# Last 256 output columns of a decoder layer: another order of token blocks, the residual added in PSUM, and the first norm's root one step earlier

## The chip, the cores and the metric

The kernel runs on one core of a Trainium2 chip. The metric is the device time of one execution in microseconds (us); the verdict compares the medians of several runs. One further execution is recorded by the profiler, and all durations of single instructions come from it. Engines are written as in the profile: PE (matrix multiply), PEld (its weight loads), DVE (vector), ACT (scalar and activation), POOL, and SP, which here only issues DMAs. ACT and POOL issue DMAs too.

## What is computed

One decoder layer over 320 tokens of width 2048: 256 of a prompt and 64 of a sample (8 sequences of 8). In the reference, cut to what matters here:

```
xn = rms_norm(x, g_mix);  z = xn @ w_in        # B, C, h, q, k, v and two gates
h  = x + merged(conv branch, window attention) @ w_o
hn = rms_norm(h, g_ffn)
h  = h + (silu(hn @ w_gate) * (hn @ w_up)) @ w_down      # inner width 5632
y  = rms_norm(h, g_final)                                # y_prompt, y_sample
```

Caches of keys, values and convolution state are returned as well. All is float32 in and out.

## The kernel before, in words

**Layout.** Activations are held transposed: 128 of the 2048 features on the partitions, 320 tokens along the free axis, 16 blocks of features. `hT` is the residual in that form. Tokens come in three blocks, `TOK`: 0-127 and 128-255 of the prompt and the 64 of the sample.

**Products.** A weight tile of 512 rows by 256 columns is loaded by SP into `wraw` (L98), copied by ACT into a rounded half `whi` (L93) and subtracted by DVE into the rest `wlo` (L94). `product` (L116) runs three matmuls for each 128x128 piece (whi with the rounded activations, whi with their rest, wlo with the rounded ones) into two PSUM buffers of 128 features by 320 tokens. The group that PE's time is made of is L134.

**Order.** Every engine has a queue that it works through in order. The framework fixes these queues at build time, from what is ready, and among the ready by the order of the program. `after(...)` (L71) ties an instruction behind marked ones of the same engine. Small work beside a product is written as a generator; `tick` advances it by one `yield` for each weight tile, with all that it issues tied behind the last matmul, the last whi and the last wlo traced so far.

**Start.** `x_load(i)` (L223) loads a group of feature blocks of x in three pieces, one for each block of tokens: all on SP but the first group's second piece, which is on ACT, followed there by g_mix (`vrow`, L231). Nine matmuls on ones warm PE up (L235). `kv_product` (L268) is the first real product: keys and values, 512 columns, nine tiles of 1, 1 and seven times 2 feature blocks. `x_prep` transposes a block of x on PE (L246), scales it on ACT into `xh_t` (L247) and on DVE into `xl_t` (L248), and copies it to `hT` (L253). `start_rest` (L327) is the side work: small loads, sums of squares, and at its end the root of the first norm (`rstd_of`, L178, with `inv_root`, L185 to L190), three diagonal matrices `dg` (L367) and three matmuls `prb` (L368) that spread the root over all partitions. The last six k/v matmuls are tied behind `prb`. Then `rb` is copied out of PSUM (L376), and kT and vT are scaled by it (L378, L380). The q product follows; behind its fourth tile SP issues two large copies of the caches from DRAM to DRAM (L427).

**End.** The inner width is worked in halves of 24 and 20 blocks. In the second half the first seven column pairs of w_down are products as above; then `to_rows` transposes each finished block back to token rows (L935), ACT sums squares (L929), and DVE multiplies by g_final into the row buffers `y_sb` (L965). At the first of these pairs `rows_so_far` also transposes blocks 14 and 15, to which this half has not been added yet, and copies them to `y_sb` (L946). The last 256 columns are computed the other way round, tokens on the partitions: `row_product(t)` (L992) gives 128 tokens by 256 columns in PSUM, 60 matmuls for a prompt block, 40 for the sample (its rounded half and its rest lie side by side as 128 rows). `finish_row` (L1010) adds the residual from `y_sb` on DVE (L1013, for the sample a second time, L1015), sums the squares, and computes the root of the final norm. The loop at L1023 takes the blocks in the order prompt 0, prompt 1, sample, scales the rows and sends them: two sends for a prompt block (512 KB each), three for the sample.

Where `inv_root` is called with one column per row it is five short steps with a change of engine on both sides of the root:

```
last["root"] = nc.scalar.activation(s, v, AF.Sqrt)
nc.vector.reciprocal(r, s)
nc.vector.scalar_tensor_tensor(s, r, -0.5, r, op0=ALU.mult, op1=ALU.mult)
nc.vector.tensor_mul(s, s, v)
```

The functions that the change touches, with the line numbers of the profile:

Of the kernel before, what the change touches and what calls it, by code (L numbers as in the profile page):

```python
# [40 lines left out]
def hybrid_layer(ctx: ExitStack, tc: tile.TileContext, a: dict, o: list):  # L41
# [133 lines left out]
    def rstd_of(ss, shape, name, pool, out=None):  # L175

        v = pool.tile(shape, F32, tag=f"rs_v{shape[1]}", name=u(name))
        nc.vector.tensor_scalar(v, ss, 1.0 / D, EPS, op0=ALU.mult, op1=ALU.add)  # L178
        return inv_root(v, shape, name, pool, out)
# [43 lines left out]
    def x_load(i):  # L223
        cs = slice(sum(XB[:i]) * P, sum(XB[:i + 1]) * P)
        for t, (t0, tn) in enumerate(TOK):
            src = a["x_prompt"][0, t0:t0 + tn, :] if t < 2 else a["x_sample"].flatten_outer_dims()
            eng = nc.scalar if i == 0 and t == 1 else nc.sync
            eng.dma_start(xs[t][:tn, cs], src[:, cs])

    x_load(0)  # L230
    nc.scalar.dma_start(vrow[0:16, :], a["g_mix"][0].rearrange("(k p) -> k p", p=P))  # L231

    wm = ps_aux("wm")
    for _ in range(9):
# [92 lines left out]
    def start_rest():  # L327
        yield
        small_loads()
        yield  # L330
        squares(0)
        yield
        yield
        squares(1)
        pw = ps_aux("pw")
        nc.tensor.transpose(pw[:, 0:56], vrow, ident[:56, :56])
        nc.vector.tensor_copy(vecs[:, 16:56], pw[:, 16:56])
        yield
        squares(2)
        nc.vector.tensor_scalar(nsink, sink_bc, -1.0, None, op0=ALU.mult)  # L340
        pe_ = ps_aux("pe_")
        nc.tensor.matmul(pe_[:NH, :WIN], rel, oh, start=True, stop=True)
        e_sb = st.tile([NH, EL], F32, name="e_sb")
        nc.vector.memset(e_sb, NEG)
        nc.vector.tensor_copy(e_sb[:, WIN - 1:2 * WIN - 1], pe_[:NH, :WIN])
        nc.gpsimd.dma_start(e_scr, e_sb)
        yield
        squares(3)
        s3 = st.tile([P, 3], F32, name="s3")
        nc.vector.tensor_reduce(s3, ss, axis=AX.X, op=ALU.add)  # L350
        pst = ps_aux("pst")
        for c in range(8):
            nc.tensor.transpose(
                pst[:, c * 16:(c + 1) * 16], srow[:, c * P:(c + 1) * P], ident[:16, :16]
            )
        nc.vector.tensor_copy(st_sb.rearrange("p c s -> p (c s)"), pst[:, 0:128])
        nc.gpsimd.dma_start(
            bias_s, bass.AP(e_scr.tensor, e_scr.offset + WIN - TS, [[EL, NH], [1, TS], [1, WIN + TS]])
        )
        yield  # L360
        yield
        r3 = rstd_of(s3, [P, 3], "r3", st)
        prb = ps_aux("prb")
        mark["rb"] = prb
        for t, (t0, tn) in enumerate(TOK):
            dg = st.tile([P, P], F32, name=f"dg{t}")
            nc.vector.tensor_scalar(dg[:tn, :tn], ident[:tn, :tn], r3[:tn, t:t + 1], None, op0=ALU.mult)  # L367
            mark["prb"] = nc.tensor.matmul(  # L368
                prb[:, t0:t0 + tn], ones[:tn, :], dg[:tn, :tn], start=True, stop=True
            )  # L370
# [507 lines left out]
    for half in range(2):  # L878
# [34 lines left out]
                    )  # L913
        if half == 1:
            ya = xp.tile([P, 2, D], F32, tag="xh", name="ya")
            yb = xp.tile([P, 2 * D + DC], F32, tag="xl", name="yb")
            y_sb = [ya[:, 0, :], ya[:, 1, :], yb[:, 0:D]]
            gfb = yb[:, D:2 * D]

            yo = yb[64:P, 2 * D:]  # L920
            nc.gpsimd.dma_start(gfb, a["g_final"].partition_broadcast(P))
            NSQ = KC - 1
            ssf = op.tile([P, 3, NSQ], F32, name="ssf")
            nc.vector.memset(ssf, 1.0)

            def row_squares(t, i, src):
                tn, n = TOK[t][1], src.shape[-1]
                jk = tmp("td", "jk")
                nc.scalar.activation(jk[:tn, :n], src, AF.Square, accum_out=ssf[:tn, t, i:i + 1])  # L929

            def to_rows(k):
                pt = ps_aux(u("fa"))
                dst = [pt[:tn, t * P:(t + 1) * P] for t, (t0, tn) in enumerate(TOK)]
                for t, (t0, tn) in enumerate(TOK):
                    nc.tensor.transpose(dst[t], hT[:, k, t0:t0 + tn], ident)  # L935
                return dst

            warm = op.tile([P, 1], F32, name="warm")
            with after(last["sig"]):
                nc.scalar.activation(warm, ones[:, 0:1], AF.Sqrt)  # L940

            def rows_so_far():

                for k in (KC - 2, KC - 1):
                    for t, src in enumerate(to_rows(k)):
                        nc.vector.tensor_copy(y_sb[t][:TOK[t][1], k * P:(k + 1) * P], src)  # L946

        for mp in range(8 if half == 0 else 7):
            c0 = mp * CW
            ps = product(  # L950
                lambda k0, n: load_cols(w_d, f0 + k0, n, c0), nf,
                lambda k: a_h[:, k, :], lambda k: a_l[:, k, :], "dn",
            )
            for c in range(2):
                k = mp * 2 + c
                nc.vector.tensor_add(hT[:, k, :], hT[:, k, :], ps[c][:, :T])
            if half == 1:
                pc = [to_rows(mp * 2 + c) for c in range(2)]
                for c in range(2):
                    k = mp * 2 + c  # L960
                    ks = slice(k * P, (k + 1) * P)
                    for t in range(3):
                        row_squares(t, k, pc[c][t])
                    for t, (t0, tn) in enumerate(TOK):
                        nc.vector.tensor_mul(y_sb[t][:tn, ks], pc[c][t], gfb[:tn, ks])  # L965
                if mp == 0:
                    rows_so_far()


    nf = FH[1]  # L970
# [21 lines left out]
    def row_product(t):  # L992

        ps = ps_acc(u("dr"))
        t0, tn = TOK[t]
        for k in range(nf):
            wh, wl = (w[:, k % KT, :] for w in held[k // KT])
            if t < 2:
                xhk, xlk = a_h[:, k, t0:t0 + tn], a_l[:, k, t0:t0 + tn]
                ms = ((xhk, wh), (xlk, wh), (xhk, wl))  # L1000
            else:
                both = a_t[:, k, t0:t0 + 2 * tn]
                ms = ((both, wh), (both, wl))
            for m, (x, w) in enumerate(ms):
                nc.tensor.matmul(  # L1005
                    ps[:, :CW], x, w, start=(k == 0 and m == 0), stop=(k == nf - 1 and m == len(ms) - 1)
                )
        return ps

    def finish_row(t, ps):  # L1010
        tn = TOK[t][1]
        y = y_sb[t][:tn, es]
        nc.vector.tensor_add(y, ps[:tn, :CW], y)  # L1013
        if t == 2:
            nc.vector.tensor_add(y, ps[tn:2 * tn, :CW], y)  # L1015
        row_squares(t, NSQ - 1, y)
        v = op.tile([P, 1], F32, name=u("vf"))
        nc.vector.scalar_tensor_tensor(
            v, ssf[:, t, NSQ - 1:NSQ], 1.0 / D, s14[:, t:t + 1], op0=ALU.mult, op1=ALU.add
        )  # L1020
        return inv_root(v, [P, 1], "rf", op)

    for t in range(3):  # L1023
        tn = TOK[t][1]
        y = y_sb[t]
        r = finish_row(t, row_product(t))[:tn]
        gl = gfb[:tn, es]
        if t < 2:
            out = y_p[0, t * P:(t + 1) * P, :]
            nc.scalar.activation(y[:, 0:DC], y[:, 0:DC], AF.Copy, scale=r)  # L1030
            nc.vector.tensor_scalar(y[:, DC:e0], y[:, DC:e0], r, None, op0=ALU.mult)
            nc.vector.scalar_tensor_tensor(y[:, es], y[:, es], r, gl, op0=ALU.mult, op1=ALU.mult)
            nc.sync.dma_start(out[:, 0:DC], y[:, 0:DC])
            nc.sync.dma_start(out[:, DC:D], y[:, DC:D])
        else:
            out = y_s.flatten_outer_dims()
            nc.scalar.activation(yo[:, 0:e0 - DC], y[:tn, DC:e0], AF.Copy, scale=r)
            h = DC // 2
            nc.vector.tensor_scalar(y[:tn, 0:h], y[:tn, 0:h], r, None, op0=ALU.mult)
            nc.sync.dma_start(out[:, 0:h], y[:tn, 0:h])  # L1040
            nc.vector.scalar_tensor_tensor(yo[:, e0 - DC:], y[:tn, es], r, gl, op0=ALU.mult, op1=ALU.mult)
            nc.scalar.dma_start(out[:, DC:D], yo)
            nc.vector.tensor_scalar(y[:tn, h:DC], y[:tn, h:DC], r, None, op0=ALU.mult)
            nc.sync.dma_start(out[:, h:DC], y[:tn, h:DC])


_INS = ['x_prompt', 'x_sample', 'cache_k', 'cache_v', 'state_conv', 'rel_bias', 'w_in', 'w_conv',
# [38 lines left out]
```

## Time and profile before

| | |
|---|---|
| median of 3 runs | 1701.68 us (1701.42 to 1701.92) |
| profiled execution, its own time | 1700.47 us |
| span in its profile, first to last instruction | 1698.7 us |
| granted TensorE clock, mean | 0.998 |
| PE busy | 1686.0 us, 11640 matmuls |
| DVE, ACT, POOL busy | 868.8, 644.6, 81.3 us |
| HBM read and written | 253.29 MB, 5.08 MB |

The profile's rows read: start (us from the span's start), duration (us), engine, line, operation, tiles written and read, shape, count, and in brackets the idle time of that engine just before, with what ended it. "q" behind an engine's name means that its queue issued a DMA. The waits list who waited for whom, and the chain is the sequence of work and waits that ended last.

### The profile page before, as it was taken

Reading aid. Unit: us, or ns where it says so; the run is one execution under the profiler, and the core shown is the slowest. Engines: PE = TensorE matmul, PEld = TensorE weight load, DVE = VectorE, ACT = ScalarE, POOL = GpSimd, SP = SyncE. Lnnn points to the kernel's source line nnn. Section 1 sums busy time; section 2 is a strip of 40 time slices with the busy share of each in tenths; the row PEclk is TensorE's granted clock in tenths of the full one; section 3 lists DMA queues with packets and bytes.
Section 4 is the critical chain, followed back from the end, with each engine's and each line's share of the span. In section 5 each row is a group of like instructions: output and inputs, shape, how many; then the busy total and the mean of one; then the engine's idle time right before and its main releaser. Section 6 shows DMA issues by size and latency. Waiting matters only on the chain.

```text
span 1698.7 us, 27819 instructions
## 1 busy us (share of the span) xinstructions
PE 1686.0 (99%) x11640; PEld 1673.2 (98%) x11640; DVE 868.8 (51%) x1259; ACT 644.6 (38%) x940; POOL 81.3 (5%) x127
## 2 busy tenths in 40 slices
PE   9999999999999999999999999999999999999997
PEld 8999999999999999999999999999999999999997
DVE  6667654444444445555454545433335555554444
ACT  6445443333333333334333333322233333333343
POOL 1001221000000001220000000000000000000000
PEclk9999999999999999999999999999999999999999
DMA  7654544554454444444444544444444444445443
GB/s 219 208 154 138 160 151 137 151 149 149 149 149 149 149 150 150 150 150 148 151 150 151 151 152 151 149 149 149 149 150 149 149 150 150 151 152 168 150 143 106
DMA packets 256654, 258.22 MB, mean 152 GB/s; under 512 B 9090, under 2 KB 251486, under 8 KB 256368
## 3 DMA queue, kind: packets, MB, share of 16 engines
q1 hardware_dynamic: 254144, 250.12, 47.6%
q0 software_dynamic: 2128, 5.92, 1.1%
q8 instruction: 91, 1.49, 0.4%
q10 hardware_dynamic: 256, 0.40, 0.1%
q14 instruction: 35, 0.29, 0.0%
HBM read 253.29 MB, written 5.08 MB: 152 GB/s over the span
## 4 chain that ended last, share of the span: by engine, by line
PE 97%; DVE 0%; issue 0%; ACT 0%; DVEq 0%; ACTq 0%
PE fu L134 18%; PE fg L134 18%; PE dn L134 17%; PE wo L134 7%; PE gc L134 7%; PE ga L134 7%; PE C L134 3%; PE B L134 3%; PE H L134 3%; PE ya L134 3%; PE yc L134 3%; PE q L134 3%; PE dr L1005 1%; PE fa L935 0%; PE po L518 0%; PE pp L505 0%
## 5 line engine op out<-in xcount | busy, mean ns | idle before, releaser
L94 DVE TENSOR_TENSOR wlo<-wraw,whi 128x1024 fp32r<-128x1024 f32 (+1 forms) x479 | 571.5, 1196 | 692.6 <-ACT whi L93 690.0
L93 ACT ACTIVATE whi<-wraw 128x1024 fp32r<-128x1024 f32 (+1 forms) x479 | 491.2, 1030 | 841.9 <-PE dn L134 192.1
L134 PE MATMUL dn<-a_t,whi 128*128 128x320 f32 x1328 | 293.4, 309 | 0.0
L134 PEld LDWEIGHTS dn<-a_t,whi 128*128 128x128 f32 x1328 | 221.5, 188 | 0.0
L134 PE MATMUL fu<-hh_t,whi 128*128 128x320 f32 x704 | 217.2, 309 | 0.0
L134 PE MATMUL fg<-hh_t,wlo 128*128 128x320 f32 x704 | 217.1, 308 | 0.0
L134 PE MATMUL fg<-hh_t,whi 128*128 128x320 f32 x704 | 217.1, 308 | 0.0
L134 PE MATMUL fg<-hl_t,whi 128*128 128x320 f32 x704 | 217.1, 308 | 0.0
L134 PE MATMUL fu<-hl_t,whi 128*128 128x320 f32 x704 | 217.0, 308 | 0.0
L134 PE MATMUL fu<-hh_t,wlo 128*128 128x320 f32 x704 | 217.0, 308 | 0.0
L134 PE MATMUL dn<-a_t,wlo 128*128 128x320 f32 x664 | 204.8, 308 | 0.0
L134 PEld LDWEIGHTS fu<-hl_t,whi 128*128 128x128 f32 x704 | 132.1, 188 | 0.1
L134 PEld LDWEIGHTS fu<-hh_t,whi 128*128 128x128 f32 x704 | 132.1, 188 | 0.1
L134 PEld LDWEIGHTS fg<-hl_t,whi 128*128 128x128 f32 x704 | 132.1, 188 | 0.0
L134 PEld LDWEIGHTS fg<-hh_t,wlo 128*128 128x128 f32 x704 | 132.1, 188 | 0.0
L134 PEld LDWEIGHTS fg<-hh_t,whi 128*128 128x128 f32 x704 | 132.1, 188 | 0.0
L134 PEld LDWEIGHTS fu<-hh_t,wlo 128*128 128x128 f32 x704 | 132.1, 188 | 0.0
L134 PEld LDWEIGHTS dn<-a_t,wlo 128*128 128x128 f32 x664 | 124.6, 188 | 0.0
L134 PE MATMUL gc<-xh_t,whi 128*128 128x320 f32 x256 | 79.5, 311 | 0.0
L134 PE MATMUL ga<-xh_t,whi 128*128 128x320 f32 x256 | 79.4, 310 | 0.0
L134 PE MATMUL ga<-xl_t,whi 128*128 128x320 f32 x256 | 79.4, 310 | 0.0
L134 PE MATMUL ga<-xh_t,wlo 128*128 128x320 f32 x256 | 79.4, 310 | 0.0
(298 smaller groups left out, 2851.3 us busy)
## 6 DMA issues: line engine op xcount, KB each, us to landing
wraw<-in_w_in_dram SPq DMA_DIRECT2D x119, 512.0 KB, 3.7
wraw<-in_w_gate_dram SPq DMA_DIRECT2D x88, 512.0 KB, 3.6
wraw<-in_w_up_dram SPq DMA_DIRECT2D x88, 512.0 KB, 3.6
wraw<-in_w_down_dram SPq DMA_DIRECT2D x88, 512.0 KB, 3.5
wraw<-in_w_o_dram SPq DMA_DIRECT2D x32, 512.0 KB, 3.5
wraw<-in_w_in_dram SPq DMA_DIRECT2D x34, 256.0 KB, 4.3
wraw<-in_w_conv_out_dram SPq DMA_DIRECT2D x16, 512.0 KB, 3.5
wraw<-in_w_attn_out_dram SPq DMA_DIRECT2D x32, 256.0 KB, 3.9
```

The lines of the kernel that those rows point to most:

```text
L93: last["hi"] = nc.scalar.activation(hi, src, AF.Copy)
L94: last["lo"] = nc.vector.tensor_sub(lo, src, hi.bitcast(F32))
L134: last["mm"] = nc.tensor.matmul(ps[c][:, :T], w[:, k, c * P:(c + 1) * P], x(kc), start=(kc == 0 and i == 0), stop=(kc == nk - 1 and i == 2),)
L1005: nc.tensor.matmul(ps[:, :CW], x, w, start=(k == 0 and m == 0), stop=(k == nf - 1 and m == len(ms) - 1))
```

## The change

Three parts.

- **The end.** The blocks go in the order prompt 0, sample, prompt 1. `rows_so_far` is gone. Instead `row_product` begins, for a prompt block, by transposing the residual of blocks 14 and 15 straight into the PSUM buffer, and the product accumulates on it; for the sample the two transposes go through another PSUM buffer and DVE copies them to `y_sb`. `finish_row` sums squares from PSUM for the prompt blocks, without adds. The first two blocks are sent in two pieces each; the last one, now a prompt block, in four, all on SP. The sample no longer has a second row buffer.
- **The root.** `rstd_of` for the first norm stands one `yield` earlier; `dg` and `prb` stay where they were.
- **The loads.** The sample's pieces of the first two groups of x are issued by ACT instead of SP, and g_mix is issued ahead of the first pieces of x.

```diff
-            eng = nc.scalar if i == 0 and t == 1 else nc.sync
+            eng = nc.scalar if (i, t) in ((0, 1), (0, 2), (1, 2)) else nc.sync
...
+    nc.scalar.dma_start(vrow[0:16, :], a["g_mix"][0].rearrange("(k p) -> k p", p=P))
     x_load(0)
-    nc.scalar.dma_start(vrow[0:16, :], a["g_mix"][0].rearrange("(k p) -> k p", p=P))
...
         yield
-        yield
         r3 = rstd_of(s3, [P, 3], "r3", st)
+        yield
         prb = ps_aux("prb")
...
-                if mp == 0:
-                    rows_so_far()
...
         ps = ps_acc(u("dr"))
         t0, tn = TOK[t]
+        for c in range(2):
+            res = hT[:, KC - 2 + c, t0:t0 + tn]
+            if t < 2:
+                nc.tensor.matmul(
+                    ps[:, c * P:(c + 1) * P], res, ident, start=c == 0, stop=False, is_transpose=True
+                )
+            else:
+                pt = ps_aux(u("fa"))
+                nc.tensor.transpose(pt[:tn, 0:P], res, ident)
+                nc.vector.tensor_copy(y_sb[t][:tn, e0 + c * P:e0 + (c + 1) * P], pt[:tn, 0:P])
...
-                    ps[:, :CW], x, w, start=(k == 0 and m == 0), stop=(k == nf - 1 and m == len(ms) - 1)
+                    ps[:, :CW], x, w, start=(t == 2 and k == 0 and m == 0),
+                    stop=(k == nf - 1 and m == len(ms) - 1),
...
-        y = y_sb[t][:tn, es]
-        nc.vector.tensor_add(y, ps[:tn, :CW], y)
+        y = ps[:tn, :CW]
         if t == 2:
+            y = y_sb[t][:tn, es]
+            nc.vector.tensor_add(y, ps[:tn, :CW], y)
             nc.vector.tensor_add(y, ps[tn:2 * tn, :CW], y)
...
+    for t in (0, 2, 1):
...
+        mul = lambda a0, a1: nc.vector.tensor_scalar(y[:, a0:a1], y[:, a0:a1], r, None, op0=ALU.mult)
+        act = lambda a0, a1: nc.scalar.activation(y[:, a0:a1], y[:, a0:a1], AF.Copy, scale=r)
+        send = lambda a0, a1: nc.sync.dma_start(out[:, a0:a1], y[:, a0:a1])
+        if t == 1:
+            mul(0, 256)
+            act(1024, 1408)
+            send(0, 256)
+            send(1024, 1408)
+            mul(256, 1024)
+            act(1408, e0)
+            send(256, 1024)
         else:
...
+            mul(0, 1024)
+            act(1024, e0)
+            send(0, 1024)
+        nc.vector.scalar_tensor_tensor(y[:, es], yl, r, gl[:tn], op0=ALU.mult, op1=ALU.mult)
+        send(1408 if t == 1 else 1024, D)
```

More of the change, by code (lines that the diff above doesn't have):

```diff
@@ L360, in start_rest @@
         yield
+        r3 = rstd_of(s3, [P, 3], "r3", st)
         yield
-        r3 = rstd_of(s3, [P, 3], "r3", st)
         prb = ps_aux("prb")
@@ L915, in hybrid_layer @@
             ya = xp.tile([P, 2, D], F32, tag="xh", name="ya")
[L916 to L920, printed above, removed]
+            yb = xp.tile([P, 2, D], F32, tag="xl", name="yb")
+            y_sb = [ya[:, 0, :], ya[:, 1, :], yb[:, 0, :]]
+            gfb = yb[:, 1, :]
             nc.gpsimd.dma_start(gfb, a["g_final"].partition_broadcast(P))
@@ L940, in hybrid_layer @@
                 nc.scalar.activation(warm, ones[:, 0:1], AF.Sqrt)
[L942 to L946, printed above, removed]
         for mp in range(8 if half == 0 else 7):
@@ L1020, in finish_row @@
         )
-        return inv_root(v, [P, 1], "rf", op)
-    for t in range(3):
+        return y, inv_root(v, [P, 1], "rf", op)
+    gl = gfb[:, es]
+    for t in (0, 2, 1):
         tn = TOK[t][1]
[L1025 to L1034, printed above, removed]
-        else:
[L1036 to L1044, printed above, removed]
+        y = y_sb[t][:tn]
+        yl, r = finish_row(t, row_product(t))
+        r = r[:tn]
+        out = y_p[0, t * P:(t + 1) * P, :] if t < 2 else y_s.flatten_outer_dims()
+        mul = lambda a0, a1: nc.vector.tensor_scalar(y[:, a0:a1], y[:, a0:a1], r, None, op0=ALU.mult)
[9 more added lines that the diff above has]
+            send(256, 1024)
+        else:
+            mul(0, 1024)
[3 more added lines that the diff above has]
+        send(1408 if t == 1 else 1024, D)
 _INS = ['x_prompt', 'x_sample', 'cache_k', 'cache_v', 'state_conv', 'rel_bias', 'w_in', 'w_conv',
```

## The prediction

> **What bounds the kernel now.** I read the page first, for what is busy; then the rows of PE in order of time, for where it isn't; then the chain at each such place.
>
> ```profile
> PE 1686.0 (99%) x11640; PEld 1673.2 (98%) x11640; DVE 868.8 (51%) x1259; ACT 644.6 (38%) x940; POOL 81.3 (5%) x127
> PE 97%; DVE 0%; issue 0%; ACT 0%; DVEq 0%; ACTq 0%
> ```
>
> TensorE is the bound: it is busy 99% of the span and makes 97% of the chain that ended last. In the stretches between 60 and 1640 us its busy time equals the stretch to within 0.05 us. So the change can only gain where PE stands still, before 60 us and after its last matmul, or by giving PE less work. It touches three such places.
>
> The first is the end of the k/v product. PE rows between 42 and 48 us:
>
> ```profile
> 42.87 0.31 PE L289 MATMUL kv<-xh_t,wlo 128*128 128x320 f32 x1
> 44.98 1.04 PE L368 MATMUL prb<-dg,ones 128*128 128x128 f32 x6 [1.80 <-DVE dg L367]
> 45.95 0.41 PE L289 MATMUL kv<-xh_t,whi 128*128 128x320 f32 x1
> ...
> 46.79 0.31 PE L289 MATMUL kv<-xh_t,wlo 128*128 128x320 f32 x1
> 47.13 0.41 PE L134 MATMUL q<-xh_t,whi 128*128 128x320 f32 x1
> ```
>
> Matmuls of this form start 0.147 us apart when nothing holds them. From 42.87 to 44.98 PE waits for dg, the diagonal made of the first norm's root: 2.11 - 0.15 = 2.0 us lost. At 47.13 another 0.34 - 0.15 = 0.2 goes (0.3 by the weight loads, "PEld q L134 <- DVE kT L378" among the waits): the q product needs a buffer that kT frees, and kT needs rb, which is copied from prb. Why dg is late stands in ScalarE's rows:
>
> ```profile
> 34.90 0.53 ACT L247 ACTIVATE xh_t<-pt,vecs 128x320 fp32r<-128x320 f32 x1 [0.62 <-PE pt L246]
> 37.78 0.53 ACT L247 ACTIVATE xh_t<-pt,vecs 128x320 fp32r<-128x320 f32 x1 [2.36 <-PE pt L246]
> ...
> 40.73 1.28 ACT L185 ACT_TABLE_LOAD   x1
> 42.02 0.21 ACT L185 ACTIVATE r<-r 128x3 f32<-128x3 f32 x1
> ```
>
> The root starts at 40.43 (DVE row L178, queued behind the 1.22 us split L94 of the last weight tile), pays a table load of 1.28, and its four small DVE steps (L186 to L190) then alternate with three wlo splits of 0.66 to 0.69 us, so that r is done at 44.4 and dg at 45.2.
>
> The second place is the tail:
>
> ```profile
> 1690.04 0.42 DVE L1013 TENSOR_TENSOR yb<-dr,yb 64x256 f32<-64x256 f32 x1 [1.46 <-PE dr L1005]
> 1690.49 0.43 DVE L1015 TENSOR_TENSOR yb<-dr,yb 64x256 f32<-64x256 f32 x1
> 1691.01 0.42 ACT L929 ACTIVATE jk<-yb 64x256 f32<-64x256 f32 x1 [2.30 <-DVE yb L1015]
> ...
> 1692.76 0.48 DVE L1039 TENSOR_SCALAR yb<-yb,rf 64x512 f32<-64x512 f32 x1
> ...
> 1694.29 0.50 SPq L1044 DMA_DIRECT2D out_dram<-yb  x1
> ```
>
> The last product ends at 1690.0. Two adds take it to 1690.95; squares, root and refinement last from 1691.01 to 1692.74 (1.75 with the hand-over); three scalings lead to the last send at 1694.29. SP's closing waits for the sends last 2.5 us in two pieces behind that issue, so the last one lands at about 1697.4, and 1.3 us of closing follow.
>
> The third is the start, where PE waits for weight tiles:
>
> ```profile
> 4.08 0.89 SPq L259 DMA_DIRECT2D wraw<-in_w_in_dram  x2
> 9.28 0.63 ACT L93 ACTIVATE whi<-wraw 128x512 fp32r<-128x512 f32 x1 [1.41 <-DMA wraw<-in_w_in_dram]
> 9.97 0.42 PE L289 MATMUL kv<-xh_t,whi 128*128 128x320 f32 x1 [0.32 <-ACT whi L93]
> ```
>
> The second tile is issued at 4.08 and lands 5.2 us later; the weight loads wait 0.6 us for its split.
>
> **Part 1: the root one step earlier.** The side work advances once per weight tile and is tied, engine by engine, behind the last split traced so far. Now the root sits in the last tile's step, behind that tile's wlo (ends 40.52). One step up it is tied behind the wlo of the tile before (34.31 to 35.54). It moves one DVE step, a table load, one ACT step and four DVE steps; no DMA, and nothing on SP or POOL. Where it lands there is room: ACT idles 2.36 us ahead of 37.78, and 1.28 + 0.21 = 1.49 fits; DVE idles 1.74 ahead of 38.34, and four steps at 0.2 us apart fit. So r is ready by about 38 us. What is late next is dg: three DVE steps, 0.64 us, still behind the last wlo, so done by 41.2 to 42.3, depending on whether xl_t (L248, 0.55) and its copy go first. PE needs prb at the earliest after its twelve matmuls for the first two column blocks, about 42.4. So the 2.0 us goes. With prb no longer last, rb and kT (0.49 each) lie beside the remaining nine matmuls (1.3 us), so the 0.3 goes too. I take 2.3; bounds 0 (dg still last) and 2.6 (the prb matmuls also close up, 1.04 now for what takes about 0.8).
>
> Does it come back? The q tiles behind the cache copies (L427) are the danger: their loads land late, and the split of the fifth q tile is done at 57.7 to 58.9 (ACT) while PE reaches that tile at 62.3. Starting 2.3 earlier leaves 1 us and more. From 60 us on nothing else but PE bounds, so it stays.
>
> **Part 2: the tail.** PE's work: rows_so_far goes, six transposes in the first down pair. That pair's column takes 18.95 us against 18.28 for the next (the stretches between first transposes), so 0.67 for six. Six transposes come in front of the row products. Net 0; bounds -0.2 and +0.3 (a transpose row after a dr row starts 0.29 instead of 0.12 later once in the trace). The six copies on DVE become two. No wait on PE is added: blocks 14 and 15 of hT have been final since the first half.
> The order of products doesn't change their sum: 60 matmuls each for the prompt blocks, 40 for the sample, so PE still ends at 1690.0. Behind it:
> - the two adds (1690.04 to 1690.95) fall away, since the squares read PSUM: chain starts at 1690.08, r is in use at 1690.08 + 1.75 = 1691.83. From PSUM an activation of 128x128 takes 0.26 (jk<-fa) and one of 256 from SBUF 0.42, so I leave 0.42.
> - mul(0,256): from 0.62 for 768 and 0.48 for 512 columns, 0.34; first send at 1692.20.
> - act of 384 columns: from 1.15 for 1024 and 0.93 for 768, 0.6 each, done 1692.43 and 1693.05; mul(256,1024) 0.62, done 1692.8; the last product with g 0.48, done 1693.3.
> - four issues on SP at 0.43 each: 1692.2, 1692.6, 1693.05, 1693.5.
> - The bytes: 1 MB instead of the sample's 0.5. The sends at 1688.61 and 1688.98 carried 1 MB in 2.6 and 3.6 us to landing, so 3.95 from first issue to last landing: 1692.2 + 3.95 = 1696.15. The last send alone, at 1693.5 + 2.6, gives 1696.1.
> Against 1697.4 that is 1.25 us. Bounds: -0.5 (a loss, if the 5.0 us median of the pair issued at 1681.5 holds) and 1.7.
>
> **Part 3: the loads.** SP loses two issues, 0.59 and 0.48, so that the first w_in tile goes 0.6 and the second up to 1.07 earlier. ACT gains two, ahead of its table load at 1.67, which is needed at 5.57 only; g_mix ahead of x moves that x piece from 0.74 to 1.19, landing 3.3 later at 4.5, and its transposes start at 5.77: hidden. g_mix itself isn't waited for, since PE warms up until 5.5. The gain is bounded by what PE waits: 0.6 at the second tile, 0.5 at the third. Against it: SP already waited 1.6 us in three pieces for x pieces to land before it could issue (L259), and the DMA share between 14 and 24 us is 1.07, at 280 GB/s, so tiles landing there come no earlier than bytes allow. Between 2 and 7 us the share is 0.87 and 0.73: some room. I take 0.3; bounds -0.2 and 1.1.
> [...]
>
> **The sum.** 2.3 + 1.25 + 0.3 = 3.85 us. The profiled execution took 1700.47 (span 1698.7, 1.8 around it) and would take 1696.6; the median of the runs is 1701.68, 1.2 above it, so I predict 1701.68 - 3.85 = 1697.8. A difference of 0.2% (3.4 us) is about what a measurement of this kernel can tell from no change.
>
> **Rivals.**
> - Loads bound by bytes: part 3 gives nothing, 1698.1. For it: share 1.07 from 14 us on. Against: the shares before. 20%. [...]
> - The root moves but prb stays late (dg behind the q splits, or ACT's order puts the root behind the last split), or PE's lead is lost to q tiles landing at 57 us: part 1 gives 0, 1700.1. Against: ties and gaps above. 13%.
> - A straggling send: the pair of 1681.5 had an instruction fetch (queue q8, one packet) in its stretch and landed at a median of 5.0 instead of 3.1. Some 1.8 us more: 1699.6. 10%.
> - Slower: the sample's second x piece, now on ACT, is queued behind ACT's first activations, which end at 7.88, instead of ahead of them. With the 4.7 us to landing of its old row it comes at 12.6, PE wants it at 8.86 and stands 3.7 us, of which 0.5 is idle there anyway. At the end of the trace the granted clock is 0.50 from 3.4 us after the last matmul, so a stand of over 3.4 (landing after 12.3) also halves the clock. At the start the six transposes at 5.77 took 1.54, against 0.49 for three at 8.86, warm-up from 1.60 not yet through; some 5.5 us at half speed cost 2.7. Then 3.2 + 2.7 - 3.55 = +2.4: 1704.0. Against: ACT's split of tile 0 already runs ahead of activations that the program names first, so its order follows readiness. 4%.
> - More than forecast: part 3 gives 0.9, part 2 1.7: 1696.7. 8%.
> The forecast as worked out has 45%. Faster by over 0.2% (below 1698.3): 43 + 14 of the first rival's 20 + 8 = 65%. Within: 31%. Slower: 4%. The range 1696.5 to 1699.8 takes in the forecast, the first rival, the straggler and the last case: 83%.
>
> **What would show it.** Part 1: the table load near 36 us, prb directly behind a kv row with no idle, q's first row near 44.8. Part 2: no add behind the last dr row, squares 0.1 after it, first send 2.2 after it, end 1.25 earlier relative to PE's end. Part 3: the second w_in issue near 3.2, no idle ahead of the row now at 9.97. Wrong would be a table load still behind 40 us, a PE gap near 62 us, or a last landing over 4.5 us after the first of the four sends.

## The result and the profile after

| | before | after |
|---|---|---|
| median of the runs, us | 1701.49 (1701.42 to 1701.92, 7 runs) | 1695.93 (1695.81 to 1697.41, 7 runs) |
| ratio, 95% interval | | 0.997 (0.9959 to 0.998) |
| profiled execution, us | 1700.47 | 1696.12 |
| its span, us | 1698.7 | 1694.4 |

The change makes the kernel 5.56 us faster by the medians, in the direction forecast, but the 3.85 us of the sum are too few and 1695.93 lies below the range, which ended at 1696.5. The two profiled executions are only 4.35 us apart. So there are two things to explain: how the 4.35 divides into the three parts, and where the medians find another 1.2 us that this pair of profiles doesn't show.

The bound is the same, from the page of the changed kernel:

```profile
PE 1685.1 (99%) x11640; PEld 1673.3 (99%) x11640; DVE 867.4 (51%) x1253; ACT 644.0 (38%) x941; POOL 81.5 (5%) x127
PE 99%; DVE 0%; issue 0%; ACT 0%; DVEq 0%; ACTq 0%
```

TensorE now makes 99% of the chain that ended last, 97% before. PE rows around the diagonal's product:

```profile
40.99 0.31 PE L289 MATMUL kv<-xl_t,whi 128*128 128x320 f32 x1
41.14 0.31 PE L289 MATMUL kv<-xh_t,wlo 128*128 128x320 f32 x1
41.28 0.97 PE L368 MATMUL prb<-dg,ones 128*128 128x128 f32 x6
42.18 0.41 PE L289 MATMUL kv<-xl_t,whi 128*128 128x320 f32 x1
...
43.75 0.31 PE L289 MATMUL kv<-xh_t,wlo 128*128 128x320 f32 x1
43.90 0.35 PE L134 MATMUL q<-xh_t,whi 128*128 128x320 f32 x1
```

Look at the distances of the starts: 0.15, 0.14, then prb with no idle in brackets. The 2.0 us stand is gone, and q follows its last kv row after 0.15, without the loss of before. ScalarE's rows show why:

```profile
33.89 0.53 ACT L247 ACTIVATE xh_t<-pt,vecs 128x320 fp32r<-128x320 f32 x1 [0.62 <-PE pt L246]
34.44 1.28 ACT L185 ACT_TABLE_LOAD   x1
35.73 0.20 ACT L185 ACTIVATE r<-r 128x3 f32<-128x3 f32 x1
36.77 0.53 ACT L247 ACTIVATE xh_t<-pt,vecs 128x320 fp32r<-128x320 f32 x1 [0.84 <-PE pt L246]
```

Table load and root stand in the gap that the prediction named: the idle time ahead of the second activation is 0.84 instead of 2.36. The tail, all engines:

```profile
1686.46 0.28 PE L1005 MATMUL dr<-wlo,a_t 128*128 128x256 f32 x1
...
1686.84 0.38 ACT L927 ACTIVATE jk<-dr 128x256 f32<-128x256 f32 x1 [3.76 <-PE dr L1005]
...
1688.55 1.12 ACT L1034 ACTIVATE ya<-ya,rf 128x384 f32<-128x384 f32 x2 [0.81 <-DVE rf L190]
1688.56 0.88 DVE L1033 TENSOR_SCALAR ya<-ya,rf 128x256 f32<-128x256 f32 x2
1688.93 1.80 SPq L1035 DMA_DIRECT2D out_dram<-ya  x4
1689.47 0.48 DVE L1048 SCALAR_TENSOR_TENSOR ya<-dr,rf,yb 128x256 f32<-128x256 f32 x1
```

The last product ends at 1686.74, the squares begin 0.1 later with no add between, the first of four sends goes 2.19 after the product. In the trace their landings are at 1690.78, 1691.36, 1692.41 and 1693.14. From PE's end to the span's end it is 7.62 us; before, 8.69. The start, SyncE's issues, and the first stretch of the k/v product:

```profile
1.21 0.41 SPq L259 DMA_DIRECT2D wraw<-in_w_in_dram  x1
1.66 0.91 SPq L228 DMA_DIRECT2D x<-in_x_prompt_dram  x2
3.56 0.81 SPq L259 DMA_DIRECT2D wraw<-in_w_in_dram  x2
```

The second weight tile is issued at 3.56 instead of 4.08. Of the 2.72 us between 7.28 and 10.00, PE was busy for 2.40 before and for all of it after (time, then PE, PEld, DVE, ACT, POOL with instruction counts, then clock, DMA share, GB/s; the first line is before, the second after):

```profile
7.28:10.00 2.72, 2.40 (x17) 2.12 (x16) 1.84 (x5) 1.25 (x3) 0.00 (x0) 1.00 0.85 248
7.28:10.00 2.72, 2.72 (x20) 2.71 (x19) 2.39 (x5) 1.59 (x4) 0.00 (x0) 1.00 0.92 316
```

This pair suggests that the loads took away the stand at the second tile; further runs, under part 3 below, show that it is another one.

With marks at the same instruction in both traces the 4.35 us divide so. The transposes into pw (L336) load their first weights at 25.95 before and 24.94 after: 1.0 by the loads in this pair.

```profile
25.95 0.13 PEld L336 LDWEIGHTS pw<-ident,vrow 56*128 56x128 f32 x1 [0.19 <-issue]
24.94 0.13 PEld L336 LDWEIGHTS pw<-ident,vrow 56*128 56x128 f32 x1 [0.19 <-issue]
```

The first weights of q: 47.13 and 43.83, 3.3, so 2.3 by the root. PE's end: 1690.01 and 1686.74, still 3.3, so nothing in between is given back and the transposes cost nothing net. The rest is the tail, 1.07.

### The profile page after: what moved, and what is told of

Its sections match the earlier page's. It is cut to its first block, busy times and chain, and to the rows that moved or that the text cites. A ratio compares the mean times of both kernels' runs of the same rounds, so it can differ in the third digit from the quotient of the medians.

```text
span 1694.4 us, 27814 instructions
## 1 busy us (share of the span) xinstructions
PE 1685.1 (99%) x11640; PEld 1673.3 (99%) x11640; DVE 867.4 (51%) x1253; ACT 644.0 (38%) x941; POOL 81.5 (5%) x127
## 4 chain that ended last, share of the span: by engine, by line
PE 99%; DVE 0%; issue 0%; ACT 0%; DVEq 0%; ACTq 0%
PE fu L134 18%; PE fg L134 18%; PE dn L134 17%; PE wo L134 7%; PE gc L134 7%; PE ga L134 7%; PE C L134 3%; PE B L134 3%; PE H L134 3%; PE ya L134 3%; PE yc L134 3%; PE q L134 3%; PE kv L289 2%; PE dr L1005 1%; PE pt L246 0%; PE po L518 0%
```

## The experiments

The first four asked where the 1.2 us are that the profiles don't show: in the start (theory S), in the last sends (E), or in the chance of a few runs of the kernel before (N). Timed beside them, that kernel took 1700.92 (1699.72 to 1702.34, 33 runs).

**again**: the kernel before, unchanged.

> The kernel before, unchanged, for a second profile. Its timed runs (1701.5) stood 1.2 us further above its span (1698.7) than those of the changed kernel stand above theirs. If that 1.2 us is lost at the start (theory S: weight tiles that land later than in the one profiled execution), this span is near 1699.7 and PE's transposes of the small vectors (pw, at 25.95 in the first profile) come near 27. If it is lost in the last sends (theory E), the last landing comes 8.5 us after PE's end instead of 7.4. If neither (theory N: the profiled execution only differs by chance), the span is 1698.7 again and time minus span 1.8.

Measured: 1701.08 (1699.6 to 1701.87), ratio 1.0002 (0.9993 to 1.0011), span 1699.4. Its pw mark lies at 25.46, not near 27 as S has it, and its last landing 7.43 us behind PE's end, not 8.5 as E has it.

**root_only**: one part of the change alone.

```diff
         yield
-        yield
         r3 = rstd_of(s3, [P, 3], "r3", st)
+        yield
```

> Only the first norm's root is one yield earlier. All theories: PE's wait ahead of prb is gone, table load near 36 us, and the time falls by 2.3 us (ratio 0.9986). If q tiles that land late behind the cache copies took something back, it falls by less, with a PE gap near 62 us.

Measured: 1697.64 (1697.47 to 1699.17), 0.9983 (0.9974 to 0.9992), span 1695.7. That is 3.28 by the medians, 1 us more than the 2.0 + 0.3 that PE stood, though the interval alone (1.4 to 4.4 us) doesn't tell the two apart.

**loads_only**: the other edit at the start, alone.

```diff
-            eng = nc.scalar if i == 0 and t == 1 else nc.sync
+            eng = nc.scalar if (i, t) in ((0, 1), (0, 2), (1, 2)) else nc.sync
...
-    x_load(0)
     nc.scalar.dma_start(vrow[0:16, :], a["g_mix"][0].rearrange("(k p) -> k p", p=P))
+    x_load(0)
```

> Only the loads are moved: the sample's first two pieces of x on ACT, g_mix ahead of x. Theory S: 2.2 us less than before by the timed runs (ratio 0.9987). Theories E and N: 1.0 us less, as the two profiles show (pw at 24.94 instead of 25.95), ratio 0.9994. My prediction had 0.3.

Measured: 1700.31 (1698.95 to 1701.17), 0.9997 (0.9988 to 1.0005), so 0.61 by the medians, where nothing can be told from chance.

**end_only**: the rest of the change (row products, their order, the last sends), the start as before.

> Only the end is changed: order prompt 0, sample, prompt 1, residual in PSUM, four last sends, no rows_so_far. Theories S and N: 1.1 us less (ratio 0.9994), as the two profiles show between PE's end and the span's end (8.7 against 7.6). Theory E: 2.2 us less (0.9987). PE's own end is where it was in all three.

Measured: 1699.88 (1698.65 to 1700.55), 0.9993 (0.9984 to 1.0002, which holds 1 as well); from PE's end to the span's end 7.61. By the medians it is 1.04, as much as the tail gained in the traces.

So by the medians the extra microsecond lies with the root, and none of the three theories had put it there. What again's trace shows in the same place as the prediction's PE rows led on:

```profile
42.39 0.31 PE L289 MATMUL kv<-xh_t,wlo 128*128 128x320 f32 x1
44.48 1.28 PE L368 MATMUL prb<-dg,ones 128*128 128x128 f32 x6 [1.78 <-DVE dg L367]
45.69 0.63 PE L289 MATMUL kv<-xh_t,whi 128*128 128x320 f32 x1
46.12 0.47 PE L289 MATMUL kv<-xl_t,whi 128*128 128x320 f32 x1
46.39 0.47 PE L289 MATMUL kv<-xh_t,wlo 128*128 128x320 f32 x1
```

It is the same kernel, with the same 1.94 us stand (42.39 + 0.15 to 44.48), but behind prb the matmuls start 0.27 apart and not 0.147. The table by stretches has the reason in the third column from the right, the granted clock:

```profile
42.30:44.90 2.60, 0.82 (x7) 0.59 (x5) 2.28 (x9) 0.48 (x1) 0.00 (x0) 1.00 0.92 282
44.90:46.90 2.00, 2.00 (x9) 1.76 (x8) 1.07 (x3) 0.00 (x0) 0.00 (x0) 0.56 0.92 330
46.90:49.00 2.10, 2.10 (x11) 2.10 (x11) 2.02 (x6) 1.15 (x2) 0.00 (x0) 0.60 0.70 279
```

The trace's clock record puts it at 0.50 from 45.15 for 3.41 us. About twelve matmuls, each 0.12 late, make some 1.4 us (an estimate). PE counts as busy all that time, so no idle time and no wait shows it. The profile that the prediction was made from has a clock of 1.00 from 7.2 us to 1693.4, behind its last matmul; again, loads_only and end_only have the fall (at 45.15, 45.52 and 46.48), and root_only, without the stand, has not. The second stretch in the prediction's profile, then in root_only:

```profile
44.90:46.90 2.00, 1.92 (x12) 1.70 (x12) 1.09 (x4) 0.00 (x0) 0.00 (x0) 1.00 0.40 126
44.90:46.90 2.00, 2.00 (x15) 2.00 (x15) 2.00 (x6) 0.55 (x2) 0.00 (x0) 1.00 1.03 352
```

The times of the kernel before fall into two groups accordingly: 16 of the 33 runs lie between 1699.72 and 1700.58 (median 1699.88), 17 between 1700.92 and 1702.34 (median 1701.14), 1.26 apart. The profiled execution, at 1700.47, was one of the lower group; all three runs of the stated median were of the upper. The mean clock that is on record for each timed run, to three places, goes with the groups: over the 91 timed runs of the kernel before, these and those beside the later runs, 0.997 stands beside 19 of the 48 upper runs and one of the 43 lower, 0.999 beside none of the upper and five of the lower. In the 87 runs of kernels without the stand, or with work put into it, 0.997 doesn't occur.

That is theory C, the clock: the stand costs what it stands, and on top, in about half of the executions, 3.41 us at half clock. The next runs, on another chip, tested it (before: 1701.06, 1699.55 to 1702.1, 27 runs; 9 of them in the lower group with a median of 1699.97, 18 in the upper with 1701.29; the groups nearly meet here, at 1700.59 and 1700.80).

**fill_stall**: the kernel before, with work of no use in the stand. It adds eight matmuls whose product nobody reads, and leaves the root late.

```diff
+        fl = ps_aux("fl")
+        for _ in range(8):
+            nc.tensor.matmul(fl, busy[:, :P], busy, start=True, stop=True)
         prb = ps_aux("prb")
```

> The kernel before with the late root, but eight matmuls on ones (a PSUM buffer that nobody reads) ahead of prb, so that PE works through most of the 2.0 us that it waits for dg. The wait itself stays and one kv matmul slips behind prb (0.15 us). Theory C (clock): the wait lets the granted clock fall to half for 3.4 us in most executions, at some 1.4 us, and root_only's gain beyond 2.3 us is that. Then the clock row shows 1.00 throughout, and the time falls by about 0.9 us against the median of before (ratio 0.9995), with a narrower spread. Theory D: root_only gains its last microsecond in some other way (a shorter chain behind the root). Then the time is the same or 0.1 us longer, and the spread is that of before.

Measured: 1700.03 (1699.6 to 1701.81, ten of eleven at or below 1700.44), 0.9997 (0.9988 to 1.0006), span 1698.7. PE rows and stretches:

```profile
42.63 1.90 PE L365 MATMUL fl<-busy 128*128 128x512 bf16 x7
...
45.02 1.04 PE L371 MATMUL prb<-dg,ones 128*128 128x128 f32 x6 [0.19 <-DVE dg L370]
45.99 0.41 PE L289 MATMUL kv<-xh_t,wlo 128*128 128x320 f32 x1
46.24 0.31 PE L289 MATMUL kv<-xh_t,whi 128*128 128x320 f32 x1
```

```profile
44.90:46.90 2.00, 1.88 (x12) 1.73 (x13) 1.09 (x4) 0.00 (x0) 0.00 (x0) 1.00 0.46 150
46.90:49.00 2.10, 2.10 (x15) 1.95 (x14) 2.10 (x7) 1.16 (x2) 0.00 (x0) 1.00 0.67 246
```

prb waits for dg as long as before, to 45.02, and nothing else is earlier. Yet the median falls by 1.03 to that of the lower group, and the upper group is all but gone: one run of eleven, against 18 of 27. None of the eleven has a mean clock of 0.997; nine of the 27 have. That speaks against theory D, by which the time and the spread would be those of before. The interval of the ratio still holds 1, because the groups make it wide; the evidence is the clock of 1.00, the pitch of 0.15 and the distribution together.

**root_loads** and **root_end**: root_only with the loads, and with the end.

> The changed kernel without its new end: root earlier and loads moved. Against root_only this is the loads alone on a kernel without the clock's fall. From the four starts of before (pw at 25.3 to 25.95, mean 25.5) and the two of the moved loads (24.9 and 25.5, mean 25.2): 0.3 us less than root_only, 3.6 less than before, if parts add up. If the two first profiles were right: 1.0 us less than root_only.

> The changed kernel without its moved loads: root earlier and the new end. Against root_only this is the end alone: 1.07 us less by the profiles (8.70 to 7.62 between PE's end and the span's end), so 4.3 to 4.4 less than before; the prediction had 1.25.

Measured: 1696.91 (1696.62 to 1697.47), 0.9977 (0.9968 to 0.9986), and 1696.79 (1695.94 to 1697.75), 0.9977 (0.9967 to 0.9987). By the medians they are 4.15 us faster (3.6 expected) and 4.27 (4.3 to 4.4 expected), against the lower group of these runs 3.06 and 3.18. The times of root_loads are narrow (0.85 us), those of root_end are not (1.81, with a mean clock of 0.999 in its three slowest runs), so not every spread comes from the clock.

**after_again**: the changed kernel.

> The changed kernel on the same chip as its parts. If parts add up (root 3.3 with the clock, loads 0.3, end 1.07): 4.7 us less than before on this chip. The first comparison gave 5.6 there, with a before that stood at 1701.4 to 1701.9 in all seven runs: by theory C a phase in which its clock fell every time.

Measured: 1696.06 (1695.64 to 1696.48), 0.9972 (0.9962 to 0.9983). By the medians it is 5.00 us faster (4.7 expected); against the lower group of these runs 3.91, against the upper 5.23.

The last runs, on a third chip (before: 1700.39, 1699.77 to 1702.75, 31 runs; 18 in the lower group with a median of 1700.07, 13 in the upper with 1701.48), put the stand back into the changed kernel and took up its tail.

**loads_end**: the changed kernel with the root where it was (the diff of root_only reversed).

> The change without the move of the root, so that the 2.0 us stand ahead of prb is back. By the clock theory (the stand brings the clock to half for 3.41 us in most executions) the times are 0.7 (loads) + 0.9 (end) = 1.6 us below the kernel before by median, and spread over more than 1.5 us again; the trace shows PE waiting about 2 us for dg and, if the window falls so, matmul rows 0.27 instead of 0.15 us apart behind prb. If the parts were not additive (each one alone hidden by the root's lateness), the median would be within 0.5 us of the kernel before.

Measured: 1699.62, ten runs between 1699.44 and 1699.95 and one at 1698.23; 0.9994 (0.9985 to 1.0002). The expected 1.6 against the median of before was missed (0.77), since here ten of eleven runs fell into the upper group, and of the kernel before only 13 of 31; the expected spread of over 1.5 rests on the one other run. The mean clock is 0.999 in that run and 0.998 in the ten. Group against group it is 1701.48 - 1699.62 = 1.86 and 1700.07 - 1698.23 = 1.84, the latter from that one run. So a median of such a kernel depends on how often the fall comes, and only groups can be compared.

**loads_end_fill**: the same with the eight matmuls of fill_stall.

> The same with eight more matmuls on a tile of constants in the stand ahead of prb; their product is read by nobody. PE still waits for dg. By the clock theory the median falls by another 0.9 to 1.0 us against the run without them, to about 2.6 us below the kernel before, the spread goes, and no part of the trace from 40 to 51 us shows the clock below 1.0. By the rival (the stand itself costs the 3.3 us, the clock nothing) the two runs have the same median.

Measured: 1698.32 (1697.9 to 1700.07, ten of eleven at or below 1698.54), 0.9987 (0.9978 to 0.9996). It is 1.30 below loads_end (0.9 to 1.0 expected) and 2.07 below the kernel before (2.6 expected, with loads_end's missed 1.6 in it). The stretches of loads_end, then of loads_end_fill:

```profile
42.30:44.90 2.60, 0.98 (x7) 0.83 (x7) 1.72 (x7) 0.00 (x0) 0.00 (x0) 1.00 0.70 223
44.90:46.90 2.00, 2.00 (x10) 1.77 (x10) 1.87 (x5) 0.84 (x2) 0.00 (x0) 0.69 0.90 300
46.90:49.00 2.10, 2.10 (x10) 2.10 (x9) 2.10 (x5) 0.31 (x1) 0.00 (x0) 0.50 0.51 214
```

```profile
42.30:44.90 2.60, 2.40 (x15) 1.52 (x12) 1.70 (x7) 0.00 (x0) 0.00 (x0) 1.00 0.78 242
44.90:46.90 2.00, 2.00 (x14) 1.85 (x14) 1.89 (x5) 0.80 (x2) 0.00 (x0) 1.00 1.00 369
46.90:49.00 2.10, 2.10 (x17) 2.10 (x16) 2.10 (x5) 0.36 (x1) 0.00 (x0) 1.00 0.55 235
```

Both load prb's first weights at the same time, 43.88 and 43.87, and PE's ends are 1690.31 and 1688.93: 1.38 us for the clock alone, 1.30 by the medians. In a second kernel, on a third chip, C is borne out. The rival, that the stand itself costs the 3.3, is out.

**two_sends**: the changed kernel, whose last block is scaled in two pieces and sent in two.

```diff
-            mul(0, 256)
-            act(1024, 1408)
-            send(0, 256)
-            send(1024, 1408)
-            mul(256, 1024)
-            act(1408, e0)
-            send(256, 1024)
+            mul(0, 1024)
+            act(1024, e0)
+            send(0, 1024)
...
-        send(1408 if t == 1 else 1024, D)
+        send(1024, D)
```

> The changed kernel with the last block's rows scaled in two pieces and sent in two (1024 + 1024 columns) instead of four. If the four sends are worth what the prediction gave them (first issue at 2.2 us after the last matmul instead of about 2.8, four pieces side by side), this is 0.3 to 0.6 us slower than the changed kernel. If the bytes of 1 MB set the landing, whatever the pieces, it is the same to 0.2 us.

Measured: 1696.39 (1695.98 to 1698.2), 0.9977 (0.9968 to 0.9985). Its profiled execution was its slowest run, late at the start, so only its tail is read: 7.87 us from PE's end, 0.25 more than with four sends.

```profile
1691.11 0.89 SPq L1035 DMA_DIRECT2D out_dram<-ya  x2
1691.11 0.48 DVE L1044 SCALAR_TENSOR_TENSOR ya<-dr,rf,yb 128x256 f32<-128x256 f32 x1
```

The first issue goes 2.60 after the product instead of 2.19, but the last landing comes 3.93 behind it instead of 4.21. The 0.25 lies between the two expectations, nearer to the first. By the medians it is 0.33 against after_again, from another chip, but only 0.07 against act_send below, which ran on the same chip and has the changed kernel's tail of 7.62. So the traces give four sends 0.25 us, by the earlier first issue, of which a part is lost again in the transfers; the times can't tell it from chance.

**act_send**: the changed kernel, whose third send is issued by ScalarE.

```diff
-            send(256, 1024)
+            nc.scalar.dma_start(out[:, 256:1024], y[:, 256:1024])
```

> The changed kernel with the third of its four last sends issued by ScalarE instead of SyncE. If the queue of issues on one engine sets the last landing, the last issue comes 0.35 us earlier and the time falls by 0.3 us. If the bytes set it, the end stays where it was, to 0.1 us.

Measured: 1696.32 (1695.85 to 1696.56), 0.9976 (0.9966 to 0.9986); 7.62 us from PE's end, as in the changed kernel. The third row is from its start, where PE waits for a q tile.

```profile
1689.21 1.41 SPq L1035 DMA_DIRECT2D out_dram<-ya  x3
1689.74 0.36 ACTq L1043 DMA_DIRECT2D out_dram<-ya  x1
...
63.45 0.41 PE L134 MATMUL q<-xh_t,wlo 128*128 128x320 f32 x1 [0.96 <-DVE wlo L94]
```

The last issue comes 3.27 us after the product instead of 3.60, and the last landing 6.41 instead of 6.40. The second expectation was right: an earlier issue brings nothing in this tail. That the transfers ahead of it set the end fits this, but one trace of each kernel is all there is. None of these runs is faster than the changed kernel.

## Why the prediction was wrong, by its steps

**The step that failed** is the carrying over in the sum: "the median of the runs is 1701.68, 1.2 above it, so I predict 1701.68 - 3.85 = 1697.8". It took the 1.2 us between the profiled execution and the median for something that the change leaves alone. By the groups and the runs with work in the stand it was the half clock behind the stand at prb, which the profiled execution happened not to have, and it goes with the stand. From the profile itself the sum gave 1696.6; the changed kernel's profiled execution took 1696.12. The profile alone could not show the fall. But the 1.2 us were a number that had no row, and a rival should have asked which part of the change could take it away.

**The condition for the fall** was wrong too. The slower rival let only a stand of over 3.4 us halve the clock, read off the trace's end. Here a stand of 1.94 us did it. The 3.4 was the value of one trace: in the 14 profiles of this case the clock falls between 1.98 (root_only) and 5.15 us (root_loads) after the last matmul.

**Part 1, the root**: right. root_only is 1699.88 - 1697.64 = 2.24 faster than the lower group, and the marks give 2.3, as predicted. The table load came at 34.44 (near 36 expected). The rival in which prb stays late did not happen, and in the changed kernel's profile the lead kept its 3.3 us to PE's end. It is not safe in every execution: the profile of act_send, which loads q's first weights earliest (43.22), stands 0.96 us at 63.45 for a q tile behind the cache copies, the danger that the prediction named and gave 1 us and more of room. To 2.24 come the 1.26 to 1.41 between the groups, for the executions that had the fall.

**Part 2, the tail**: the mechanism was right, the size slightly large: 1.07 in the traces against 1.25, and in the medians root_end gives 1699.97 - 1696.79 = 3.18, so 0.94 beside the root's 2.24. The first send was as predicted, 2.19 for 2.2; the term that was off is the time from it to the last landing, 4.21 against 3.95, and in act_send this time did not follow the queue of issues (last issue 0.33 us earlier, last landing 6.41 us after the product for 6.40). The transposes cost nothing net: the first down pair's stretch fell from 18.95 to 18.29 and the last one with the row products grew from 20.11 to 20.80. No send straggled.

**Part 3, the loads**: mis-sized, though inside its bounds (0.3; -0.2 to 1.1), and not at the place that was named. In the medians root_loads gives 1699.97 - 1696.91 = 3.06, so 0.8 beside the root's 2.24 from another chip; loads_only's own interval holds 0. In the traces the mark at pw lies between 25.27 and 26.00 in the six kernels with the old loads, and at 24.33 to 25.48 in seven of the eight with the new ones (two_sends' late execution has 26.74); the middles are 0.7 apart. The second issue came 0.5 earlier (3.56, not 3.2).

But the stand at the second tile, which the prediction read as what PE could gain, is no sign of the old loads: loads_only still has it (0.31, 7.28 to 10.00), and again, the kernel before itself, has not (busy 2.72 of 2.72). What the kernels differ in lies behind it: from 10 to 18 us PE stands 0.55 or less in five of the six with the old loads (0.20, 0.19, 0, 0.49, 0.55) and 1.16 in fill_stall, and in none of the eight with the new ones. The prediction had said that the tiles of 14 us and later could come no earlier than their bytes allow.

The rival of bytes would have made this part 0. As far as the marks show, moving two issues off SP's queue was worth 0.7 to 0.8 us.

The three terms as measured, 2.24 + 0.94 + 0.8 = 4.0, stand beside 3.91 for the whole change against the lower group. The 3.85 was right for an execution without the fall, in part by luck: the tail's 0.3 too much and the loads' 0.5 too little offset each other. (The sum of the rival "more than forecast", 4.9 us, gives 1696.8, not 1696.7. The 3.55 in the slower rival is 2.3 + 1.25, with nothing for the loads.) With the fall's 1.3 it is 5.2; the 5.56 of the result, whose seven runs of the kernel before were all above 1701.4, leave 0.3, which is within what the upper group's medians differ between chips (1701.14 to 1701.48).

**What stays open** is when the fall comes. On the three chips 17 of 33, 18 of 27 and 13 of 31 runs of the same kernel were in the upper group, and ten of eleven of loads_end. In the four traces with a fall it begins 0.67, 1.02, 1.97 and 1.75 us after the stand's end, so at no fixed distance from it. In the one trace with the stand, no work in it and no fall, the prediction's, a step of 3.4133 us (the fall's length), counted on from the start of the full clock (7.18), ends at 44.73, 0.25 us before the stand does. But end_only, which has the fall (at 46.48), has a step's end inside its stand too: 46.48 - 3.41 = 43.07, with the stand from 42.56 to 44.51. What decides is not shown by these traces. Nor was the shortest stand that still brings the fall tried.

## What to carry to other kernels

- A stand of TensorE in the middle of full work can cost more than its length: here 2.0 us of waiting, and then a loss of 1.3 to 1.4 us at half clock in about half the executions of the kernel before, and in ten of eleven of loads_end. Where the times of a kernel fall into two groups, look for a granted clock below 1 behind such a stand, and profile more than one execution.
- A gap between the profiled execution and the median is no constant. Before a sum is carried from one to the other, say what the gap is and whether the change touches it.
- If the late operand can't be brought forward, a few matmuls on a tile of constants in the stand can keep the clock: in the two kernels here the traces show it at 1.00 from 40 to 51 us; the matmuls took 1.03 and 1.30 us off the median, and fill_stall's lies within 0.1 us of the lower group's.

## What the runs showed of the hardware that was not expected

- The granted clock fell to 0.50 after a stand of 1.94 us, for 3.413 us (again). In the records, it changes at multiples of one step: the full clock ahead of the fall lasts 40.960 us (loads_only, end_only, loads_end) or 37.547 (again), that is 12 and 11 times 3.4133, and behind it 1645.224, 482 times. Behind the last matmul it falls after 1.98 to 5.15 us, differently in each of the 14 profiles.
- While the clock is at half, matmuls of 128x320 start 0.267 us apart (again, 46.12 to 47.19), at full clock 0.147: 1.8 times, not 2.
- The square root began 0.01 us after its table load of 1.28 us ended (34.44 + 1.28, 35.73). The load had no other cost in this place.
- Eight matmuls without a reader, 1.55 us of TensorE's time (42.63 to 44.18), kept the clock and left prb (45.02; 44.98 in the prediction's profile) and q's first weights (47.17; 47.13) where they were.
